# Merging triangular inverses with narrow products and stacked transfers, and a norm tail with its root on ScalarE

## The chip, the cores and the metric

The kernel runs on 1 core of one Trainium2 chip. The metric is the device time of one execution in microseconds. Time before: 1188.06 us, the median of 3 runs (1185.7 to 1188.26).

A core has TensorE (PE, with its weight loads shown apart as PEld), VectorE (DVE), ScalarE (ACT), GpSimd (POOL) and SyncE (SP). SP and ACT also issue the DMA transfers, each from a queue of its own, in program order.

## The reference, cut to what matters

One layer of an encoder for 1024 tokens of width 1024 in float32: a norm, one wide projection, a mixer of two halves (gated DeltaNet with 4 heads of 128, and a short gated convolution), an output projection, a second norm, a SwiGLU of width 2816, and a final norm. Two places of it matter here. The first is the inverse in the chunked delta rule (chunk = 64):

```python
lmat = jnp.where(strict, jnp.einsum('bhncd,bhnmd->bhncm', k_beta, k) * decay, 0.0)
tmat = lax.linalg.triangular_solve(lmat, eye, left_side=True, lower=True, unit_diagonal=True)
u = jnp.einsum('bhncm,bhnme->bhnce', tmat, v_beta)
w = jnp.einsum('bhncm,bhnmd->bhncd', tmat, k_beta * jnp.exp(g)[..., None])
```

`tmat` is the inverse of a unit lower triangular 64x64 matrix, one for each head and chunk (4 heads x 16 chunks). The second is the end of the kernel, the final norm:

```python
y = x32 * lax.rsqrt(jnp.mean(x32 * x32, axis=-1, keepdims=True) + RMS_EPS)
```

## The kernel before, in words

**Order of the work.** Up to the output projection of the first 512 tokens the order is set by a planner inside the kernel (`Sim`, lines 298 to 523). Tasks run as coroutines with priorities (`PR`, line 43); each asks for an operation, and the planner hands operations out by its own cost table and the time at which it expects their data, with 0.6 us added for PE (`MARGIN`, line 41). `ecopy` and `dma2` let it choose between ACT and DVE, or SP and ACT. The result is a fixed order for each engine. PE's background work is `fill` (line 939): dense products 128x128 by 128x512 in three passes, called `acc` here, whose three PSUM banks other tasks evict. All smaller work is put between them. Behind the planner the order is written out by hand: the rest of the output projection, the SwiGLU and its down projection by a seven-product scheme (`dn`), and the tail.

**The inverses.** Tokens are handled in two halves of 512 (`hf`), each as 4 tiles of 128 tokens, so two chunks of 64 to a tile. For each head `stage_a` (line 1096) forms `kk`, k times k transposed, scales and masks it into `L` (128 x 4 x 128), and sends the four 32x32 diagonal blocks of each tile to DRAM (`dl`). `gdn` (line 1214) reads all blocks back with one block to a partition (64 partitions, 32x32 each, tile `A`), inverts them on DVE by 30 steps of two operations (the elimination), and writes the inverses to DRAM (`dx`, lines 1234 to 1243). Then `merge` (line 1176) runs for each head. It reads the inverse blocks into the diagonal of a tile `xbd` that was zeroed once, in four transfers, one for each strip r of 32 rows; transposes it block by block on DVE into `Tt`; and completes the 64x64 inverses. With `L` masked to its lower left quarters (line 1136), P is `L` times `Tt`, Q is `xbd` times P, and Q is added to `Tt`: eight float32 products of 128 columns for each head, and one copy of P from PSUM. Then come u and w from the reference with `Tt`, and the scan over chunks (A, K and O), which carries the state S from chunk to chunk, and `output` (y).

**Pool slots.** Tiles with the tags `A` and `qs` have one slot each, used in turn by the blocks, their scratch, and the scan's V and q tiles. The four `xbd` tiles are reused later for weights of the output projection (`take_lx`, line 1381).

**The tail.** In the last down-projection chunk (`LASTC`), `add_out` (line 2045) adds each finished 128x512 product to `xo`, and for a finished half row takes the sum of squares on ACT. Once both halves of a tile are there, POOL (DVE for the last tile) adds them, POOL raises the sum to the power -0.5, and `final` (line 2064) scales both halves by it and by the norm weights `nfb`, and stores them. For tile 7, the last, the weights of one half are multiplied in early and its scaling is done on ACT; everything else is scaled on DVE and stored from SP. `settle` (line 2080) puts each `final` two products behind its add, and what is left at the end is flushed in order: tile 6, then tile 7.

Of the kernel before, what the change touches and what calls it, by code (L numbers as in the profile page):

```python
# [17 lines left out]
P = 128  # L18
# [35 lines left out]
def kernel(  # L54
# [79 lines left out]
    def flat(ap):  # L134
        return ap.rearrange("p a b -> p (a b)")
# [4 lines left out]
    def bc1(row, n):  # L140
        return row.unsqueeze(1).to_broadcast([row.shape[0], n, row.shape[1]])
# [50 lines left out]
    def dma(out, in_):  # L192
        SP.dma_start(out=out, in_=in_)

    def dma2(out, in_):
        kw = dict(out=out, in_=in_)
        mover[0].either([("sp", "dma_start", nc.sync.dma_start, (), kw), ("act", "dma_start", nc.scalar.dma_start, (), kw)])
# [898 lines left out]
    def stage_a(hf, h, dl, T, dec):  # L1096
        st = sc_[hf]
        sim.wait(lambda: all((x, h, hf) in done for x in "kq") and h in dec)
        qk = qkT[h, hf]
        kv_, qv = qk[:, 0, :], qk[:, 1, :]  # L1100
        hcol = lambda n: st[n][:, :, h]
        at, L, WQ, egl = (dec[h][n] for n in ("at", "L", "WQ", "egl"))
        kt = gt("kt")
        qd = WQ[:, :, 64:192]
        pk = bank(chb, "kT")
        for t in range(4):
            tr(pk[:, tsl(t)], kv_[:, tsl(t)])
        ecopy(flat(kt), pk)
        ss = gt("ss", (P, 2, 4))
        junk = gt("jk", (P, P), BF16)  # L1110
        for t in range(4):
            ACT.activation(junk, pk[:, tsl(t)], AF.Square, accum_out=ss[:, 0, t:t + 1])
        free(pk)
        pkk = bank(chb, "kk")
        for t in range(4):
            mm(pkk[:, tsl(t)], kv_[:, tsl(t)], kv_[:, tsl(t)])
        nk, rk, av, bv, nav = (gt(t, (P, 4)) for t in ("nk", "rk", "av", "bv", "nav"))
        bk = gt("bk", (P, 4))
        DVE.tensor_scalar(nk, ss[:, 0, :], EPS, None, ALU.add)
        DVE.reciprocal(av, nk)  # L1120
        rsqrt_pow(rk, nk, 4)
        DVE.tensor_tensor(av, av, hcol("beta"), ALU.mult)
        DVE.tensor_scalar(nav, av, -1.0, None, ALU.mult)
        for t in range(4):
            DVE.scalar_tensor_tensor(L[:, t, :], pkk[:, tsl(t)], nav[:, t:t + 1], L[:, t, :], ALU.mult, ALU.mult)
        free(pkk)
        for r in range(4):
            dma(dl[h * 16 + r * 4:h * 16 + r * 4 + 4, :].rearrange("t (a b) -> a t b", a=32),
                L[32 * r:32 * r + 32, :, 32 * r:32 * r + 32])
        T[h] = dict(egl=egl, bk=bk, kt=kt, WQ=WQ, L=L, at=at, bv=bv)  # L1130
        done.add(("L", hf, h))
        DVE.tensor_tensor(bk, av, hcol("eG"), ALU.mult)
        DVE.tensor_tensor(bv, rk, hcol("beta"), ALU.mult)
        for t in (nk, rk, av, nav):
            free(t)
        DVE.tensor_tensor(L, L, bc1(offm, 4), ALU.mult)
        DVE.tensor_tensor(qd, v3(qv, 4), qd, ALU.mult)
        pqk = bank(chb, "qk")
        for t in range(4):
            mm(pqk[:, tsl(t)], kv_[:, tsl(t)], qv[:, tsl(t)])  # L1140
        DVE.tensor_tensor(sw(at), sw(v3(pqk, 4))[:, :, ::-1, :], sw(at), ALU.mult)
        free(pqk)
        pq = bank(chb, "qT")
        for t in range(4):
            tr(pq[:, tsl(t)], qv[:, tsl(t)])
        free(qk)
        live[0] -= 1
        for t in range(4):
            ACT.activation(junk, pq[:, tsl(t)], AF.Square, accum_out=ss[:, 1, t:t + 1])
        free(pq)  # L1150
        free(junk)
        nq = gt("nq", (P, 4))
        ec = EPS * 128.0
        DVE.tensor_scalar(nq[0:64, :], ss[64:128, 1, :], EPS, ec, ALU.add, ALU.mult)
        DVE.tensor_scalar(nq[64:128, :], ss[0:64, 1, :], EPS, ec, ALU.add, ALU.mult)
        free(ss)
        T[h]["nq"] = nq
        done.add(("a", hf, h))
# [14 lines left out]
        free(bv)  # L1173
        done.add(("vt", hf, h))

    def merge(hf, h, T, dx):
        st, t_ = sc_[hf], T[h]
        u = us[hf]
        for r in range(4):
            dma2(xbd[h][32 * r:32 * r + 32, :, 32 * r:32 * r + 32],  # L1180
                dx[h * 16 + r * 4:h * 16 + r * 4 + 4, :].rearrange("t (a b) -> a t b", a=32))
        Tt = gt("Tt")
        sim.wait(lambda: ("a", hf, h) in done)
        DVE.transpose(flat(Tt), flat(xbd[h]))
        pP = bank(chb, "P")
        for t in range(4):
            mm(pP[:, tsl(t)], t_["L"][:, t, :], Tt[:, t, :])
        ecopy(flat(t_["L"]), pP)
        free(pP)
        pQ = bank(chb, "Q")  # L1190
        for t in range(4):
            mm(pQ[:, tsl(t)], xbd[h][:, t, :], t_["L"][:, t, :])
        DVE.tensor_tensor(flat(Tt), flat(Tt), pQ, ALU.add)
        free(pQ)
        DVE.tensor_tensor(t_["L"], t_["kt"], bc2(t_["bk"], P), ALU.mult)
        free(t_["bk"])
        sim.wait(lambda: ("vt", hf, h) in done)
        pu = bank(chb, "u")
        for t in range(4):
            mm(pu[:, tsl(t)], Tt[:, t, :], u[:, h, t, :])  # L1200
        ecopy(flat(u[:, h]), pu)
        free(pu)
        pw = bank(chb, "w")
        for t in range(4):
            mm(pw[:, tsl(t)], t_["L"][:, t, :], Tt[:, t, :])
        free(t_["L"])
        free(Tt)
        ecopy(t_["WQ"].rearrange("p t (c n) -> p t c n", c=4)[:, :, 0:4:3, :],
                 pw.rearrange("p (t c n) -> p t c n", t=4, c=2))
        free(pw)  # L1210
        DVE.tensor_tensor(t_["kt"], t_["kt"], bc2(st["kd"][:, :, h], P), ALU.mult)
        done.add(("uw", hf, h))

    def gdn(hf):
# [28 lines left out]
        dma(dx, flat(A))  # L1243
        free(A)
        free(tmp)
        for h in heads:
            sim.spawn(merge, PR["m"], hf, h, T, dx)
        sim.wait(lambda: all(("uw", hf, h) in done for h in heads))
        for h in heads:
            sim.spawn(zload, PR["out"], hf, h)  # L1250
# [130 lines left out]
    def take_lx(n):  # L1381
        def take():
            sim.wait(lambda: all(("uw", 1, h) in done for h in heads))
            return gt("L", (P, HT), F32R), gp.tile([P, HT], F32R, name=nm("wu"), tag=f"xbd{n}", bufs=1)
        return take

    def take_wq():
# [29 lines left out]
    def coordinator():  # L1417
# [10 lines left out]
        s_ctx.__exit__(None, None, None)  # L1428
        pools["g"] = tc.tile_pool(name="gp", bufs=2, side="left", reuse_waits="tile")
        gp = pools["g"].__enter__()  # L1430
        for i in range(4):
            xbd.append(gp.tile([P, 4, P], F32, name=f"xbd{i}", tag=f"xbd{i}", bufs=1))
        for t in xbd:
            POOL.memset(t, 0.0)
        done.add("gp")
        sim.wait(lambda: "filled" in done and live[0] == 0 and all(("vt", 1, h) in done for h in heads) and
                 all(("sc", i, hf) in done and ("z", i, hf) in done for i in range(4) for hf in range(2)))
# [580 lines left out]
    block(NP, 0)  # L2018
    first_mats(3, "B21", None)
    block(NP, 1)  # L2020
    flush()
    xq_ctx.__exit__(None, None, None)
    dq = ctx.enter_context(tc.tile_pool(name="dq", bufs=1, side="right", reuse_waits="tile"))
# [21 lines left out]
    def add_out(ci, s, i, ps):  # L2045
        an = STEPSD[s][1]
        hf, ch = ADDS[an]
        t = 4 * hf + i
        cs = slice(ch * HT, (ch + 1) * HT)
        DVE.tensor_tensor(xo[t][:, cs], xo[t][:, cs], ps, ALU.add)  # L2050
        if ci < LASTC or an not in ("A12", "S4", "S3", "A22"):
            return
        st = fst[t]
        junk = dp.tile([P, HT], BF16, name=nm("jf"), tag="jf", bufs=2)
        ACT.activation(junk, xo[t][:, cs], AF.Square, scale=1.0 / 32.0, accum_out=st[:, ch:ch + 1])
        if an in ("A12", "S3"):
            POOL.tensor_scalar(st[:, ch:ch + 1], st[:, ch:ch + 1], EPS, None, ALU.add)
            if t == NT - 1:
                DVE.tensor_tensor(xo[t][:, cs], xo[t][:, cs], nfb[:, cs], ALU.mult)
        else:  # L2060
            (DVE if t == NT - 1 else POOL).tensor_tensor(st[:, 2:3], st[:, 0:1], st[:, 1:2], ALU.add)
            rsqrt_pow(st[:, 3:4], st[:, 2:3], 1)

    def final(t):
        for ch in (1, 0):
            cs = slice(ch * HT, (ch + 1) * HT)
            dst = outs[t * P:(t + 1) * P, cs]
            if t == NT - 1 and ch == 1:
                ACT.activation(xo[t][:, cs], xo[t][:, cs], AF.Copy, scale=fst[t][:, 3:4])
                ACT.dma_start(out=dst, in_=xo[t][:, cs])  # L2070
            else:
                DVE.scalar_tensor_tensor(xo[t][:, cs], xo[t][:, cs], fst[t][:, 3:4], nfb[:, cs], ALU.mult, ALU.mult)
                dma(dst, xo[t][:, cs])
# [6 lines left out]
    def settle(k):  # L2080
        while adds and adds[0][0] <= k:
            _, (ci, s, i), ps = adds.pop(0)
            add_out(ci, s, i, ps)
            if ci == LASTC and STEPSD[s][1] in ("S4", "A22"):
                finals.append((k + 2, 4 * ADDS[STEPSD[s][1]][0] + i))

    for k, (n, i) in enumerate(slots):
        ci, s = seq_d[n]
# [62 lines left out]
```

## Time and profile before

| what | value |
|---|---|
| median of the runs | 1188.06 us (1185.7 to 1188.26) |
| the profiled execution's own time | 1187.97 us |
| its span in the trace | 1186.2 us |
| granted TensorE clock over the span | 0.996 |
| PE busy | 99% of the span |
| DVE, ACT, POOL busy | 78%, 45%, 5% |
| first merge of the inverses, first P product | 205.8 us |
| second merge, first P product | 388.8 us |

A row of a timeline has the start in us, the length in us, engine, line, operation, output<-input and the count; in brackets stands the idle time before it and what ended it. A row of a tile view has the shortest, middle and longest duration in ns and the first and last start. `SPq` and `ACTq` are DMA issues on those engines. Lines 91, 92 and 442 are helpers that record every operation, so groups are told apart by their tiles.

### The profile page before, as it was taken

Reading aid. Unit: us, or ns where it says so; the run is one execution under the profiler, and the core shown is the slowest. Engines: PE = TensorE matmul, PEld = TensorE weight load, DVE = VectorE, ACT = ScalarE, POOL = GpSimd, SP = SyncE. Lnnn points to the kernel's source line nnn. Section 1 sums busy time; section 2 is a strip of 40 time slices with the busy share of each in tenths; the row PEclk is TensorE's granted clock in tenths of the full one; section 3 lists DMA queues with packets and bytes.
Section 4 is the critical chain, followed back from the end, with each engine's and each line's share of the span. In section 5 each row is a group of like instructions: output and inputs, shape, how many; then the busy total and the mean of one; then the engine's idle time right before and its main releaser. Section 6 shows DMA issues by size and latency. Waiting matters only on the chain.

```text
span 1186.2 us, 16777 instructions
## 1 busy us (share of the span) xinstructions
PE 1175.4 (99%) x5721; PEld 987.9 (83%) x5721; DVE 929.5 (78%) x1719; ACT 528.9 (45%) x1127; POOL 58.0 (5%) x95
## 2 busy tenths in 40 slices
PE   9999999999999999999999999999999999999997
PEld 8888888988888888888888888888888888888886
DVE  5998888799998798758787677767767697788676
ACT  4479832458642444224443333333333364433343
POOL 2010100001100001100000000000000000000003
PEclk8999999999999999999999999999999999999999
DMA  9942355544344535722354655455644679869413
GB/s 295 270 108 64 99 172 142 183 119 135 109 127 124 169 102 174 283 92 87 129 172 135 221 195 172 152 182 187 221 153 137 223 272 394 312 201 344 146 38 142
DMA packets 175791, 207.08 MB, mean 175 GB/s; under 512 B 21845, under 2 KB 107994, under 8 KB 175706
## 3 DMA queue, kind: packets, MB, share of 16 engines
q1 hardware_dynamic: 170328, 202.85, 52.8%
q10 hardware_dynamic: 5378, 3.16, 0.9%
q8 instruction: 45, 0.74, 0.3%
q14 instruction: 40, 0.33, 0.1%
HBM read 150.91 MB, written 55.05 MB: 174 GB/s over the span
## 4 chain that ended last, share of the span: by engine, by line
PE 96%; DVE 2%; DMA 1%; ACT 1%; issue 0%; POOL 0%; DVEq 0%; ACTq 0%; SPq 0%; POOLq 0%
PE acc L91 34%; PE acc L442 26%; PE dn L91 17%; PE o L91 4%; PE o L442 4%; PE A L442 1%; PE K L442 1%; PE ada L442 1%; PE tr L442 1%; PE ab L442 1%; PE u L442 1%; PE w L442 1%; PE qk L442 1%; PE kk L442 1%; PE O L442 1%; PE heat L91 1%
## 5 line engine op out<-in xcount | busy, mean ns | idle before, releaser
L442 PE MATMUL acc<-h,u 128*128 128x512 f32 x1200 | 300.3, 398 | 0.0
L442 PEld LDWEIGHTS acc<-h,u 128*128 128x128 f32 x1200 | 219.0, 188 | 41.7
L91 PE MATMUL acc<-h,hl 128*128 128x512 f32 x600 | 140.1, 390 | 0.0
L91 PEld LDWEIGHTS acc<-h,hl 128*128 128x128 f32 x600 | 112.4, 188 | 23.2
L91 PE MATMUL acc<-h,u 128*128 128x512 f32 x456 | 106.1, 389 | 0.0
L91 PE MATMUL acc<-T,hl 128*128 128x512 f32 x432 | 101.3, 390 | 0.2 <-ACT cc L92 0.2
L91 PEld LDWEIGHTS acc<-h,u 128*128 128x128 f32 x456 | 85.6, 188 | 17.8
L91 PEld LDWEIGHTS acc<-T,hl 128*128 128x128 f32 x432 | 80.9, 188 | 17.2 <-ACT cc L92 0.6
L92 DVE TENSOR_TENSOR xo<-xo,dn 128x512 f32<-128x512 f32 x84 | 57.2, 686 | 44.0 <-PE dn L91 35.5
L91 PE MATMUL dn<-h,h 128*128 128x512 f32 x396 | 90.7, 389 | 0.0
L91 PEld LDWEIGHTS dn<-h,h 128*128 128x128 f32 x396 | 74.3, 188 | 15.4
L92 ACT COPY cc<-acc 128x512 f32<-128x512 f32 x66 | 38.5, 591 | 108.4 <-PE acc L91 108.4
L91 PE MATMUL acc<-T,u 128*128 128x512 f32 x360 | 84.0, 389 | 0.0
L91 PEld LDWEIGHTS acc<-T,u 128*128 128x128 f32 x360 | 67.6, 188 | 14.0
L442 ACT CAST u<-raw 128x512 fp32r<-128x512 f32 x67 | 41.3, 622 | 63.6 <-PE acc L442 57.5
L92 DVE TENSOR_TENSOR cc<-cc,acc 128x512 f32<-128x512 f32 x66 | 43.9, 684 | 29.8 <-PE acc L91 29.8
L92 DVE TENSOR_TENSOR hl<-R,hl 128x512 fp32r<-128x512 f32 x60 | 39.5, 689 | 33.4 <-ACT hl L92 33.4
L442 DVE TENSOR_TENSOR u<-raw,u 128x512 fp32r<-128x512 f32 x82 | 56.2, 685 | 8.8 <-ACT u L442 8.2
L442 DVE SCALAR_TENSOR_TENSOR cv<-pr,cols_b,cv 128x512 f32<-128x512 f32 x72 | 52.9, 746 | 1.4 <-ACT cv L442 1.1
L92 ACT CAST h<-rw 128x512 fp32r<-128x512 f32 x57 | 32.7, 618 | 41.7 <-PE dn L91 34.6
L92 DVE TENSOR_TENSOR u<-R,u 128x512 fp32r<-128x512 f32 x46 | 30.1, 688 | 20.5 <-ACT u L92 20.5
L92 ACT CAST hl<-R 128x512 fp32r<-128x512 f32 x60 | 35.5, 620 | 23.8 <-DVE R L92 10.7
(339 smaller groups left out, 2033.5 us busy)
## 6 DMA issues: line engine op xcount, KB each, us to landing
raw<-in_w_in_dram SPq DMA_DIRECT2D x82, 256.0 KB, 3.4
am_scr<-cc SPq DMA_DIRECT2D x77, 256.0 KB, 4.9
raw<-in_w_ada_dram SPq DMA_DIRECT2D x56, 256.0 KB, 3.5
rw<-am_scr SPq DMA_DIRECT2D x55, 256.0 KB, 5.1
rw<-bm_scr SPq DMA_DIRECT2D x53, 256.0 KB, 5.2
bm_scr<-raw SPq DMA_DIRECT2D x51, 256.0 KB, 5.4
R<-in_w_gate_dram SPq DMA_DIRECT2D x22, 512.0 KB, 3.8
R<-in_w_up_dram SPq DMA_DIRECT2D x22, 512.0 KB, 5.1
```

The costliest lines, as they stand in the source:

```text
L91: return call(*a, **k)
L92: ins = call(*a, **k)
L442: ins = call(*a, **k)
```

## The change

It has two parts. **The merge.** The blocks in `dl` and `dx` are laid out by strip r first, then head, then tile, so that one transfer takes one strip of all heads. `xbd` is one tile for all heads (16 blocks of 128), filled by four transfers. A second tile `XA`, zeroed each time, gets the same inverse blocks, moved by 32 rows or columns, so that it pairs the blocks of two tiles of a head; a third, `DD`, gets the right-hand blocks as a stack of 32 columns and is transposed block by block on DVE. In `L` the lower left quarters of every second tile are moved beside those of its neighbour. Then only the missing quarter is computed, with 32 moving columns: P is two products for each head, Q two. Four small copies for each head place Q's quarters in `Tt`, where an add over the whole tile was before. Ten transfers replace sixteen in each half. **The tail.** For tiles 6 and 7 the root is taken on ACT with the two sums as input and bias, and the reciprocal on DVE; the table for the root is loaded early by a dummy call; half of tile 6 is scaled on ACT too, between the last add and the last square; and tile 6 is finished around tile 7's add.

```diff
@@ stage_a
         for r in range(4):
-            dma(dl[h * 16 + r * 4:h * 16 + r * 4 + 4, :].rearrange("t (a b) -> a t b", a=32),
+            dma(dl[r * 16 + h * 4:r * 16 + h * 4 + 4, :].rearrange("t (a b) -> a t b", a=32),
                 L[32 * r:32 * r + 32, :, 32 * r:32 * r + 32])
...
-        DVE.tensor_tensor(L, L, bc1(offm, 4), ALU.mult)
+        DVE.tensor_tensor(L[:, 1:4:2, :], L[:, 1:4:2, :], bc1(offm, 2), ALU.mult)
+        for c in range(2):
+            ecopy(L[64 * c:64 * c + 32, 1:4:2, 64 * c + 32:64 * c + 64], L[64 * c + 32:64 * c + 64, 0:4:2, 64 * c:64 * c + 32])
@@ merge
-    def merge(hf, h, T, dx):
+    def merge(hf, h, T, XA, DD):
...
-        for r in range(4):
-            dma2(xbd[h][32 * r:32 * r + 32, :, 32 * r:32 * r + 32],
-                dx[h * 16 + r * 4:h * 16 + r * 4 + 4, :].rearrange("t (a b) -> a t b", a=32))
+        L = t_["L"]
+        sim.wait(lambda: ("a", hf, h) in done)
+        pP = bank(chb, "P")
+        for g in range(2):
+            mm(pP[:, 32 * g:32 * g + 32], L[:, 2 * g + 1, :], DD[:, 1, 2 * h + g, :])
+        ecopy(DD[:, 0, 2 * h:2 * h + 2, :], v3(pP[:, 0:64], 2))
+        free(pP)
         Tt = gt("Tt")
-        sim.wait(lambda: ("a", hf, h) in done)
-        DVE.transpose(flat(Tt), flat(xbd[h]))
-        pP = bank(chb, "P")
-        for t in range(4):
-            mm(pP[:, tsl(t)], t_["L"][:, t, :], Tt[:, t, :])
-        ecopy(flat(t_["L"]), pP)
-        free(pP)
+        DVE.transpose(flat(Tt), flat(xbd[0][:, 4 * h:4 * h + 4, :]))
         pQ = bank(chb, "Q")
-        for t in range(4):
-            mm(pQ[:, tsl(t)], xbd[h][:, t, :], t_["L"][:, t, :])
-        DVE.tensor_tensor(flat(Tt), flat(Tt), pQ, ALU.add)
+        for g in range(2):
+            mm(pQ[:, 32 * g:32 * g + 32], XA[:, 2 * h + g, :], DD[:, 0, 2 * h + g, :])
+        for p in range(2):
+            for c in range(2):
+                q = 64 * c + 32 - 32 * p
+                ecopy(Tt[64 * c:64 * c + 32, p:4:2, 64 * c + 32:64 * c + 64], v3(pQ[q:q + 32, 0:64], 2))
         free(pQ)
+        done.add(("q", hf, h))
@@ gdn, behind the elimination and the store of dx
+        DD = gt("qs", (P, 2, 8, 32))
+        for c in range(2):
+            r0 = 32 * c + 16
+            dma(DD[64 * c:64 * c + 64, 0], dx[r0:r0 + 16, :].rearrange("(h p) (a b) -> (p a) h b", p=2, a=32))
+        XA = gt("A", (P, 8, P))
+        POOL.memset(XA, 0.0)
+        for r in range(4):
+            dma2(xbd[0][32 * r:32 * r + 32, :, 32 * r:32 * r + 32], dx[r * 16:r * 16 + 16, :].rearrange("t (a b) -> a t b", a=32))
+        for c in range(2):
+            for p in range(2):
+                q, r0 = 64 * c + 32 - 32 * p, 32 * c + p
+                dma2(XA[q:q + 32, :, q:q + 32], dx[r0:r0 + 15:2, :].rearrange("t (a b) -> a t b", a=32))
+        DVE.transpose(flat(DD[:, 1]), flat(DD[:, 0]))
         for h in heads:
-            sim.spawn(merge, PR["m"], hf, h, T, dx)
+            sim.spawn(merge, PR["m"], hf, h, T, XA, DD)
+        sim.wait(lambda: all(("q", hf, h) in done for h in heads))
+        free(XA)
+        free(DD)
@@ before the down projection
     block(NP, 1)
+    ACT.activation(warm, ones[:, 0:1], AF.Sqrt)
     flush()
@@ add_out (tail)
+        if ci == LASTC and an == "A22" and t == NT - 1:
+            DVE.reciprocal(fst[t - 1][:, 3:4], fst[t - 1][:, 2:3])
         DVE.tensor_tensor(xo[t][:, cs], xo[t][:, cs], ps, ALU.add)
+        if ci == LASTC and an == "A22" and t == NT - 1:
+            final(t - 1, (1,))
...
         if an in ("A12", "S3"):
             POOL.tensor_scalar(st[:, ch:ch + 1], st[:, ch:ch + 1], EPS, None, ALU.add)
+            if t >= NT - 2:
+                DVE.tensor_tensor(xo[t][:, cs], xo[t][:, cs], nfb[:, cs], ALU.mult)
+        elif t >= NT - 2:
             if t == NT - 1:
-                DVE.tensor_tensor(xo[t][:, cs], xo[t][:, cs], nfb[:, cs], ALU.mult)
+                final(t - 1, (0,))
+            ACT.activation(st[:, 2:3], st[:, 0:1], AF.Sqrt, bias=st[:, 1:2], scale=1.0)
+            if t == NT - 1:
+                DVE.reciprocal(st[:, 3:4], st[:, 2:3])
         else:
-            (DVE if t == NT - 1 else POOL).tensor_tensor(st[:, 2:3], st[:, 0:1], st[:, 1:2], ALU.add)
+            POOL.tensor_tensor(st[:, 2:3], st[:, 0:1], st[:, 1:2], ALU.add)
             rsqrt_pow(st[:, 3:4], st[:, 2:3], 1)
@@ final
-            if t == NT - 1 and ch == 1:
+            if t >= NT - 2 and ch == 1:
                 ACT.activation(xo[t][:, cs], xo[t][:, cs], AF.Copy, scale=fst[t][:, 3:4])
-                ACT.dma_start(out=dst, in_=xo[t][:, cs])
+                (ACT if t == NT - 1 else SP).dma_start(out=dst, in_=xo[t][:, cs])
```

The other lines of the diff make `xbd` one tile of the same total size, let its later use for weights follow, and keep tile 6 out of the list that flushes `final`.

More of the change, by code (lines that the diff above doesn't have):

```diff
@@ L1383, in take @@
             sim.wait(lambda: all(("uw", 1, h) in done for h in heads))
-            return gt("L", (P, HT), F32R), gp.tile([P, HT], F32R, name=nm("wu"), tag=f"xbd{n}", bufs=1)
+            if len(xbd) == 1:
+                xbd.append(gp.tile([P, 4, HT], F32R, name="wu", tag="xbd", bufs=1))
+            return gt("L", (P, HT), F32R), xbd[1][:, n, :]
         return take
@@ L1430, in coordinator @@
         gp = pools["g"].__enter__()
[L1431 to L1434, printed above, removed]
+        xbd.append(gp.tile([P, 16, P], F32, name="xbd", tag="xbd", bufs=1))
+        for i in range(2):
+            POOL.memset(xbd[0][:, 8 * i:8 * i + 8, :], 0.0)
         done.add("gp")
@@ L2057, in add_out, with final @@
             POOL.tensor_scalar(st[:, ch:ch + 1], st[:, ch:ch + 1], EPS, None, ALU.add)
+            if t >= NT - 2:
+                DVE.tensor_tensor(xo[t][:, cs], xo[t][:, cs], nfb[:, cs], ALU.mult)
+        elif t >= NT - 2:
             if t == NT - 1:
-                DVE.tensor_tensor(xo[t][:, cs], xo[t][:, cs], nfb[:, cs], ALU.mult)
+                final(t - 1, (0,))
+            ACT.activation(st[:, 2:3], st[:, 0:1], AF.Sqrt, bias=st[:, 1:2], scale=1.0)
+            if t == NT - 1:
+                DVE.reciprocal(st[:, 3:4], st[:, 2:3])
         else:
-            (DVE if t == NT - 1 else POOL).tensor_tensor(st[:, 2:3], st[:, 0:1], st[:, 1:2], ALU.add)
+            POOL.tensor_tensor(st[:, 2:3], st[:, 0:1], st[:, 1:2], ALU.add)
             rsqrt_pow(st[:, 3:4], st[:, 2:3], 1)
-    def final(t):
-        for ch in (1, 0):
+    def final(t, chs=(1, 0)):
+        for ch in chs:
             cs = slice(ch * HT, (ch + 1) * HT)
             dst = outs[t * P:(t + 1) * P, cs]
-            if t == NT - 1 and ch == 1:
+            if t >= NT - 2 and ch == 1:
                 ACT.activation(xo[t][:, cs], xo[t][:, cs], AF.Copy, scale=fst[t][:, 3:4])
-                ACT.dma_start(out=dst, in_=xo[t][:, cs])
+                (ACT if t == NT - 1 else SP).dma_start(out=dst, in_=xo[t][:, cs])
             else:
@@ L2084, in settle @@
             if ci == LASTC and STEPSD[s][1] in ("S4", "A22"):
-                finals.append((k + 2, 4 * ADDS[STEPSD[s][1]][0] + i))
+                t = 4 * ADDS[STEPSD[s][1]][0] + i
+                if t != NT - 2:
+                    finals.append((k + 2, t))
     for k, (n, i) in enumerate(slots):
```

## Prediction

> **What bounds the kernel now.** I read the page first (busy shares and the chain that ended last), then busy time by stage.
>
> ```profile
> span 1186.2 us, 16777 instructions
> PE 1175.4 (99%) x5721; PEld 987.9 (83%) x5721; DVE 929.5 (78%) x1719; ACT 528.9 (45%) x1127; POOL 58.0 (5%) x95
> PE 96%; DVE 2%; DMA 1%; ACT 1%; issue 0%; POOL 0%; DVEq 0%; ACTq 0%; SPq 0%; POOLq 0%
> ```
>
> PE is busy 1175.4 of 1186.2 us and makes up 96% of the chain. A busy PE need not be a fast one, so the question for each stage is whether anything but PE's own queue sets its length (columns: stretch, its length, then busy us and instructions of PE, PEld, DVE, ACT, POOL, granted clock, DMA share, GB/s):
>
> ```profile
> 200.00:220.00 20.00, 20.00 (x148) 18.72 (x147) 16.49 (x27) 6.23 (x11) 1.48 (x2) 1.00 0.54 157
> 220.00:380.00 160.00, 160.00 (x852) 136.41 (x852) 146.21 (x347) 89.21 (x246) 12.24 (x11) 1.00 0.45 127
> 380.00:410.00 30.00, 29.39 (x196) 26.33 (x196) 22.09 (x38) 13.59 (x24) 0.96 (x1) 1.00 0.62 176
> 541.00:575.00 34.00, 33.84 (x191) 28.88 (x190) 29.23 (x46) 20.07 (x38) 0.77 (x2) 1.00 0.49 162
> 575.00:1176.00 601.00, 601.00 (x2653) 497.51 (x2652) 440.82 (x668) 232.53 (x426) 7.46 (x19) 1.00 0.57 196
> 1176.00:1186.20 10.20, 2.77 (x13) 1.95 (x11) 5.38 (x9) 2.40 (x7) 2.76 (x4) 0.82 0.45 165
> ```
>
> Both merges (200 to 220 and 380 to 410) lie where PE has no idle time, but for 0.61 us in the second, and PE stays full behind them. So a PE instruction less is time less, as long as what it waits for comes no later. After 1176 PE is done; the last 8 us are add, norm, scale and store.
>
> **PE work removed.** Each merge computes P and Q for four heads.
>
> ```profile
> 203.76 2.20 PE L442 MATMUL acc<-h,u 128*128 128x512 f32 x9
> 205.81 1.95 PE L442 MATMUL P<-Tt,L 128*128 128x128 f32 x16
> L442 PE MATMUL P<-Tt,L x64: 270/275/377, 205.8 to 400.7; 128*128 128x128 f32 x64
> L442 PE MATMUL Q<-L,xbd x64: 272/275/377, 208.5 to 403.5; 128*128 128x128 f32 x64
> 104.32 0.59 PE L442 MATMUL G<-g,ct 128*128 128x16 f32 x4
> 104.76 0.71 PE L442 MATMUL acc<-h,u 128*128 128x512 f32 x2
> ```
>
> The trace has two instructions for one f32 product: 64 for the 32 P products, 64 for Q. Sixteen span 1.95 us and one lasts 0.275, so they follow each other every (1.95 - 0.275)/15 = 0.112 us. The change has half as many products, each with 32 moving columns instead of 128. What does a narrow one cost? Nearest row: G, with 16 columns, takes 104.76 - 104.32 = 0.44 us for four, 0.11 each. So width gives nothing and count gives everything: 64 instructions fewer x 0.112 = **7.1 us** less PE time, half of it in each merge. A dense product (acc) takes (205.81 - 203.76)/9 = 0.228.
>
> [...]
>
> **Transfers and their order.** The inverted 32x32 blocks go to DRAM (dx) and come back.
>
> ```profile
> 197.30 0.47 SPq L442 DMA_DIRECT2D dx<-A  x1
> 200.31 5.57 SPq L442 DMA_DIRECT2D xbd<-dx  x9
> 200.51 4.70 ACTq L442 DMA_DIRECT2D xbd<-dx  x7
> 200.34 0.95 POOL L442 MEMSET A<- 128x1024 f32 x1 [47.65 <-DMA dx<-A]
> 204.63 0.71 DVE L442 STREAM_TRANSPOSE Tt<-xbd 128x512 f32<-128x512 f32 x1 [1.50 <-DMA xbd<-dx]
> 379.57 0.47 SPq L442 DMA_DIRECT2D dx<-A  x1
> 382.49 7.14 SPq L442 DMA_DIRECT2D xbd<-dx  x8
> 388.80 3.40 PE L442 MATMUL P<-Tt,L 128*128 128x128 f32 x24
> 394.70 1.16 PE L442 MATMUL Q<-L,xbd 128*128 128x128 f32 x8 [0.48 <-ACT L L442]
> L442 SPq DMA_DIRECT2D xbd<-dx x17: 302/360/635, 200.3 to 389.2; - x17
> DMA packets 1043, 0.18 MB, mean 182 GB/s; under 512 B 880, under 2 KB 1043, under 8 KB 1043
> DMA packets 597, 0.07 MB, mean 69 GB/s; under 512 B 597, under 2 KB 597, under 8 KB 597
> ```
>
> Sixteen transfers of 128 pieces of 128 bytes become ten: two (DD) of 512 pieces, four (xbd) of 512, four (XA) of 256. That is 4096 pieces against 2048. The two packet rows are single microseconds: 1043 between 202 and 203, when the queues had a backlog, and 597 between 205 and 206. The latter is what two queues can issue: 128 pieces every 0.360 us is 356 per us and queue. With 512 pieces to an issue that limit goes, so I take the former pace.
>
> In the instruction order of the changed kernel P stands 5 dense products earlier in the first merge (behind 647 instead of 652), so at 205.81 - 5 x 0.228 = 204.67, and Q behind eight P products and one dense one, at 204.67 + 16 x 0.112 + 0.23 = 206.7. In the second merge P stands behind 1252 instead of 1240, with 3.55 us of PE already saved: 388.80 - 3.55 + 12 x 0.228 = 388.0, Q at 390.0. The last kk there moves from 1005 to 1014, so the elimination behind it and dx come 3.55 - 9 x 0.228 = 1.5 us earlier; dx lands near 381.0 instead of 382.5.
>
> First merge: dx lands at 200.3 (POOL's memset waited for just that). DD goes first on SP, with two 256 KB loads queued ahead of it instead of three. Even after the 3.4 us that the first xbd transfer needed here (200.31 to the transpose that waited for it, less one shorter load) it is in by about 203.9. DD's transpose has half the elements of the 0.71 us one, about 0.4, so P is ready at 204.4 and just meets PE. All 4096 pieces at 1043 per us, from about 202, are in by 205.9, ahead of Q at 206.7. XA must first be cleared on POOL, 0.95 us behind dx, which is done at 201.3, before its queue slot comes. Second merge: 7 us from dx to P, 9 to Q: no wait. I take 0.3 us of new waiting in the first merge and let the 0.48 us wait of Q go: together nothing. The bounds are in the rivals.
>
> Queued behind: on ACT the four XA and xbd issues stand ahead of the P copies, and the last XA on each queue waits until DD has landed; before, ACT stood behind seven such issues (4.70 us), now four. On DVE four xbd transposes and a dense eviction stand behind DD's; three banks of dense results give that eviction more than 24 x 0.228 = 5.5 us. One weight load on SP moves behind six transfers; its cast comes some 18 us later.
>
> **Small work.**
>
> ```profile
> L442 DVE TENSOR_TENSOR Tt<-Tt,Q x8: 681/681/689, 209.7 to 403.8; 128x512 f32<-128x512 f32 x8
> L442 ACT COPY L<-P x8: 579/586/603, 206.9 to 401.1; 128x512 f32<-128x512 f32 x8
> L442 ACT COPY S<-K 128x128 f32<-128x128 f32 x4 | 0.8, 280 | 2.1 <-PE K L442 2.1
> L442 ACT ACTIVATE kd<-raw 128x16 f32<-128x16 f32 x2 | 0.4, 217 | 0.5 <-DVE raw L442 0.5
> ```
>
> DVE loses eight adds (8 x 0.68 = 5.4 us) and half of eight maskings; ACT gains 32 copies of 64 elements for Q and 16 for L, each between 0.217 and 0.280, and its P copies shrink from 0.586 to the same: about 48 x 0.23 - 8 x 0.35 = 8 us more on an engine that is 45% busy. In the merge one head's four Q copies take 0.9 us; head by head PE needs 8 x 0.112 = 0.9 for u and as much for w. So ACT keeps up, hidden behind PE. If it did not, PE would wait some 0.2 us for each head.
>
> **The tail.**
>
> ```profile
> 1177.47 1.41 DVE L92 SCALAR_TENSOR_TENSOR xo<-xo,fst,nfb 128x512 f32<-128x512 f32 x2
> 1178.80 0.69 DVE L92 TENSOR_TENSOR xo<-xo,dn 128x512 f32<-128x512 f32 x1
> 1179.59 0.63 ACT L92 ACTIVATE jf<-xo 128x512 bf16<-128x512 f32 x1 [1.21 <-DVE xo L92]
> 1180.65 0.99 POOL L92 TENSOR_TENSOR fst<-fst,nhalf 128x1 f32<-128x1 f32 x1 [1.07 <-DVE fst L92]
> 1180.49 2.07 DVE L92 SCALAR_TENSOR_TENSOR xo<-xo,fst,nfb 128x512 f32<-128x512 f32 x3
> 1181.67 0.72 ACT L92 ACTIVATE xo<-xo,fst 128x512 f32<-128x512 f32 x1 [1.36 <-POOL fst L92]
> 1181.26 1.66 SPq L92 DMA_DIRECT2D out_dram<-xo  x3
> L442 ACT ACTIVATE b1c<-ada,cols_a 128x1 f32<-128x1 f32 x8 | 2.0, 252 | 0.0
> L442 DVE RECIPROCAL av<-nk 128x4 f32<-128x4 f32 x8 | 1.4, 172 | 0.0
> ```
>
> Now the three scalings on DVE end at 1182.56 and the last store is issued then. After the change tile 6's reciprocal (0.17) precedes the last add, which moves by 0.1 to 1179.6; ACT scales half of tile 6 from 1179.0 to 1179.7, so the square starts at 1179.7 instead of 1179.59. Its sum is out at 1180.4; root 0.25, reciprocal 0.17, hand-overs 0.1: 1180.9. Then ACT and DVE scale tile 7 side by side, DVE with one scaling instead of three behind the add: done by 1181.65. The last issue comes 1182.56 - 1181.65 = **0.9 us** earlier. Bounds: 0.6 if the root costs more, 1.2 if the last stores also gain from two that left sooner.
>
> **Sum.** 1187.97 (the profiled execution: span 1186.2 and 1.77 around it) - 7.1 - 0.9 = 1180.0. The median of the runs shown is 1188.06, 0.09 more, which I leave out.
>
> **Rivals.**
> *A, pieces at 597 per us* (for it: the only row with 128-byte pieces alone): 6.9 us from 201.7, so 208.6; Q waits 1.9 us in the first merge, nothing in the second (381.0 + 1.4 + 6.9 = 389.3, before 390.0). 1181.9, and up to 1185 if DD or loads get in the way of each other. 0.14.
> *B, slower: pieces at the mean pace of before.* 2048 pieces took from 200.31 to about 206.8, 315 per us, and 382.49 to 389.63 in the second, 287. 4096 at that pace need 13.0 and 14.3 us: XA lands at 213.3 and 395.3, Q waits 6.6 and 5.3 us, 11.9 in all: 1191.9. It decides from the point where the waits pass 8.0 us, a pace below some 380 per us. Against it: the 1043 row, and that issuing set that mean. 0.08. [...]
> *C, priced by columns*: if 32 columns cost a quarter of 128, the 64 instructions left save 64 x 0.084 = 5.4 more: 1174.6. The G row is against it. 0.03. [...]
> *D, hidden*: another engine holds the stages. DVE is 146.21 of 160 us busy between the merges, and if its queue set the pace the 7.1 us would be lost: 1187.1. Against it: DVE loses about as much work, and PE shows no wait there. 0.07.
>
> **How the numbers follow.** Forecast 1180.0 with 0.68 (1178 to 1182: tail and price bounds, 0.5 us of waits, and the runs' own scatter); A 0.14, B 0.08, C 0.03, D 0.07. The range leaves out B, C and D, 0.18: 1178.0 to 1185.5. Faster by over 0.2% (about what a measurement of this kernel can tell): forecast, A and C, 0.85; D within it, 0.07; B slower, 0.08.
>
> **What would show it.** P and Q at 32 instructions each, still 0.11 apart; PE busy near 1168; no idle before P or Q over 0.5 us; the last POOL power gone and the last store issued about 2.9 us after PE's end instead of 3.8. A wait of Q for XA over 2 us, or DD's transpose waiting past 205, would make it wrong.

## The result and the profile after

The changed kernel takes 1185.05 us in the median of its 22 runs, the kernel before 1186.26 on the same chips. Two of the 22 were disturbed (1891 and 4199 us); without them the median is 1184.78 and the mean 1184.5, against a mean of 1186.7 before: ratio 0.9981, 95% interval 0.9974 to 0.9989. It is faster, but by 2.2 us where 8.0 were forecast.

The page of the changed kernel, in the lines that answer to those of before:

```profile
span 1183.6 us, 16666 instructions
PE 1171.5 (99%) x5657; PEld 982.9 (83%) x5657; DVE 924.8 (78%) x1720; ACT 536.3 (45%) x1174; POOL 57.3 (5%) x92
```

PE has 64 instructions less, as forecast, but is busy 1171.5 us and not 1168. The same stages (columns as before):

```profile
200.00:220.00 20.00, 20.00 (x124) 18.73 (x123) 14.79 (x24) 9.51 (x30) 1.47 (x2) 0.83 0.64 186
...
380.00:410.00 30.00, 28.45 (x163) 25.44 (x163) 19.89 (x34) 15.80 (x41) 1.92 (x2) 0.89 0.70 182
```

Read the granted clock, third from the end: 1.00 in both merges before, 0.83 and 0.89 now. PE is full in the first merge, 20.00 of 20, and still does less. In finer stretches (stretch, length, PE busy and count, granted clock, DMA share, GB/s), at the edges of both dips:

```profile
204.00:205.00 1.00, 1.00 (x10) 1.00 0.62 236
205.00:206.00 1.00, 1.00 (x10) 0.79 0.02 6
206.00:207.00 1.00, 1.00 (x5) 0.50 0.75 272
...
212.00:213.00 1.00, 1.00 (x9) 0.79 0.87 272
```

```profile
393.00:394.00 1.00, 1.00 (x9) 0.66 0.61 194
...
400.00:401.00 1.00, 1.00 (x11) 0.93 0.00 0
```

The clock goes to exactly 0.50. The shares in the edge rows give the moments: 205.58 to 212.42 and 393.32 to 400.14, so 6.84 and 6.82 us, each losing half of itself, 3.4 us of PE's work. The timeline of the first shows what ran:

```profile
202.35 1.86 PE L442 MATMUL P<-qs,L 128*128 128x32 f32 x16
204.05 0.47 PE L442 MATMUL acc<-h,u 128*128 128x512 f32 x1
204.36 2.33 PE L442 MATMUL Q<-qs,A 128*128 128x32 f32 x16
206.51 0.77 PE L442 MATMUL acc<-h,u 128*128 128x512 f32 x1
...
207.93 1.91 PE L442 MATMUL u<-u,Tt 128*128 128x128 f32 x8
...
214.09 1.06 PE L442 MATMUL u<-u,Tt 128*128 128x128 f32 x8
```

P and Q follow each other without a gap, with one dense product between them. In the middle of Q, 3.2 us behind P's start, everything turns slow: a dense product takes 0.77 instead of 0.47, eight u instructions 1.91 instead of 1.06. PE shows no wait there. A clock that halves looks in the page like a busy PE.

The second merge has a second trouble, a wait that I had excluded:

```profile
379.62 0.49 SPq L442 DMA_DIRECT2D dx<-A  x1
383.49 1.29 SPq L442 DMA_DIRECT2D qs<-dx  x2
387.16 1.41 ACTq L442 DMA_DIRECT2D A<-dx  x2
388.61 0.62 ACT L442 CAST h<-raw 128x512 fp32r<-128x512 f32 x1 [4.48 <-DMA xbd<-dx]
389.26 0.69 DVE L442 TENSOR_TENSOR h<-raw,h 128x512 fp32r<-128x512 f32 x1 [2.88 <-ACT h L442]
389.87 0.43 DVE L442 STREAM_TRANSPOSE qs<-qs 128x256 f32<-128x256 f32 x1
390.36 1.97 PE L442 MATMUL P<-qs,L 128*128 128x32 f32 x16 [1.54 <-DVE ch L442]
```

ACT stands at its last two issues until 388.6. Behind them is a cast (h), behind the cast a subtraction on DVE, and behind that DD's transpose (qs). P starts when that transpose ends, at 390.30. DD's data was there before: its two transfers, issued at 383.5 and 384.2, took 4.1 us each, so the last landed at 388.3, and PE had no more work from 388.82 on.

The start of the kernel differs too, with nothing changed there. Before, first, then after:

```profile
16.00:18.00 2.00, 2.00 (x11) 0.50 1.12 336
```

```profile
16.00:18.00 2.00, 1.40 (x13) 1.00 1.12 335
```

Here a dip of the same depth fell in one execution and not in the other. So of the 2.6 us between the two spans, 2.2 are luck (first P at 202.35 here, at 204.51 in the experiment e1_wide, which has the start's dip and the same order up to it). The rest, by terms: products -7.1, dips 2 x 3.4 = +6.8, the wait 1.54 less the 0.61 us of idle that went = +0.9, tail -0.55; with the start -2.15. Some 0.5 us stay unassigned.

### The profile page after: what moved, and what is told of

Same layout as the page of the kernel before. It is cut to its first block, busy times and chain, and to the rows that moved or that the text cites. A ratio compares the mean times of both kernels' runs of the same rounds, so it can differ in the third digit from the quotient of the medians.

```text
span 1183.6 us, 16666 instructions
## 1 busy us (share of the span) xinstructions
PE 1171.5 (99%) x5657; PEld 982.9 (83%) x5657; DVE 924.8 (78%) x1720; ACT 536.3 (45%) x1174; POOL 57.3 (5%) x92
## 4 chain that ended last, share of the span: by engine, by line
PE 93%; DVE 4%; ACT 1%; DMA 1%; issue 1%; POOL 0%; ACTq 0%; DVEq 0%; POOLq 0%
PE acc L91 34%; PE acc L442 24%; PE dn L91 17%; PE o L91 4%; PE o L442 3%; PE K L442 1%; PE A L442 1%; PE u L442 1%; PE ada L442 1%; PE w L442 1%; DVE xo L92 1%; PE ab L442 1%; PE qk L442 1%; PE kk L442 1%; PE heat L91 1%
```

## The experiments

My theory after this comparison: the narrow products themselves cost the clock, and after some 3 us of them it is halved (0.50, from 3.2 us behind the first P's start and 3.0 us behind the second's). Rivals: the new transfers and waits do it, or the tail carries the whole gain.

| kernel | median us | ratio (95% interval) | clock of the profiled run |
|---|---|---|---|
| after | 1184.78 | 0.9981 (0.9974 to 0.9989) | 0.993 |
| e1_wide | 1180.74 | 0.995 (0.9936 to 0.9964) | 0.996 |
| e2_tail | 1186.88 | 1.0003 (0.9994 to 1.0012) | 0.997 |
| e3_merge | 1184.65 | 0.9987 (0.9974 to 1.0) | 0.995 |
| e4_before_narrow | 1189.46 | 1.0027 (1.0013 to 1.004) | 0.996 |
| e5_wide_sp | 1179.26 | 0.993 (0.9917 to 0.9942) | 0.996 |
| e6_w64 | 1182.07 | 0.996 (0.9947 to 0.9973) | 0.999 |
| e7_pwide | 1179.38 | 0.9939 (0.9926 to 0.9952) | 0.996 |
| e8_start | 1178.91 | 0.9929 (0.9916 to 0.9941) | 0.999 |
| e9_all | 1178.15 | 0.9928 (0.9917 to 0.994) | 0.999 |
| e10_all_oldtail | 1178.91 | 0.9933 (0.9921 to 0.9945) | 0.999 |
| e11_start_w64 | 1182.4 | 0.9965 (0.9951 to 0.9979) | 0.999 |
| e12_start_w32 | 1184.14 | 0.9982 (0.9973 to 0.9991) | 0.993 |

Each ratio is to the kernel before on the same chip. That kernel's median is 1185.96, 1188.07 and 1186.32 us on the three chips of the experiments, by the share of its runs that have the start's dip; its runs at a clock of 0.999 take 1185.6 to 1185.8 us in the mean on all three. A ratio carries that share. So two rows are compared by their medians, with the ratios beside them where they say something else.

### e1_wide: the same products, made wide

```diff
-            mm(pP[:, 32 * g:32 * g + 32], L[:, 2 * g + 1, :], DD[:, 1, 2 * h + g, :])
+            mm(pP[:, 128 * g:128 * g + 128], L[:, 2 * g + 1, :], bc1(DD[:, 1, 2 * h + g, :], 4))
...
-            mm(pQ[:, 32 * g:32 * g + 32], XA[:, 2 * h + g, :], DD[:, 0, 2 * h + g, :])
+            mm(pQ[:, 128 * g:128 * g + 128], XA[:, 2 * h + g, :], bc1(DD[:, 0, 2 * h + g, :], 4))
...
```

The same 32 columns are read four times over; the lines left out here let the copies read the first quarter of each result.

> The changed kernel with the products P and Q made 128 columns wide again: the same 32 columns are streamed four times (stride 0), and only the first quarter of the result is read. Instructions, order, transfers and waits stay as in the changed kernel; a product behind its own weight load takes about 0.11 us at 32 and at 128 columns. Theory 1 (narrow products keep the array idle three quarters of their time, so the granted clock falls to 0.50 in both merges for about 6.8 us each): the granted clock stays at 0.9 to 1.0 at 204 to 214 and 390 to 402 us, PE's busy time falls by 5 to 7 us against the changed kernel's 1171.5, and the time by as much, to 1178 to 1180 us, ratio 0.992 to 0.995. Rival (the missing gain lies in waits and in the ten transfers): 1184 to 1186 us, ratio 0.998 to 1.000, and the dips stay.

1180.74 us, ratio 0.995: four times the columns, and 4 us less than the changed kernel, though not quite the 1178 to 1180 us expected. Its clock and its PE rows:

```profile
206.00:208.00 2.00, 2.00 (x20) 1.00 0.45 152
...
394.00:396.00 2.00, 2.00 (x18) 1.00 0.27 88
```

```profile
204.51 1.95 PE L442 MATMUL P<-qs,L 128*128 128x128 f32 x16
206.53 1.95 PE L442 MATMUL Q<-qs,A 128*128 128x128 f32 x16
389.42 2.05 PE L442 MATMUL P<-qs,L 128*128 128x128 f32 x16 [1.71 <-DVE ch L442]
```

Both dips are gone; sixteen instructions take 1.95 us where the narrow ones took 1.86. PE's busy time is 1167.9 us, 3.6 less than after, where 5 to 7 were expected. But this execution has the start's dip, worth some 2.2 us, and that of after has not; with it the difference is 5.8. The wait before the second P stays, 1.71 us, so it is not the dips that it comes from, nor they from it. The theory holds, the rival is out. That narrow products leave the array idle for three quarters of their time is my estimate, from 32 of 128 columns in the same 0.11 us; no trace shows it.

### e4_before_narrow: the kernel before, made narrow

```diff
-            mm(pP[:, tsl(t)], t_["L"][:, t, :], Tt[:, t, :])
+            mm(pP[:, t * P:t * P + 32], t_["L"][:, t, :], Tt[:, t, 0:32])
...
-            mm(pQ[:, tsl(t)], xbd[h][:, t, :], t_["L"][:, t, :])
+            mm(pQ[:, t * P:t * P + 32], xbd[h][:, t, :], t_["L"][:, t, 0:32])
...
```

> The kernel before with all its 128 products P and Q cut to their first 32 columns (three quarters of P and of Q are left out, so the off-diagonal inverses are incomplete); transfers, order and number of instructions stay. Theory 1: the granted clock falls to 0.50 in both merges of this kernel too, where it was 1.00, for 6.8 us or more each, and the time rises by 5 to 8 us, ratio 1.004 to 1.007. Rival (width and clock have nothing to do with each other; the dips come from the new transfers or waits): the clock stays at 1.00 and the ratio is 0.998 to 1.000.

Less streamed, more time: +0.27%, 3.2 us, less than the 5 to 8 expected. The copies of P and the adds of Q are cut to the same columns, and the planner moved other work with them, which I had not expected (the second merge's first P stands at 382.02 instead of 388.80), so this is the price of the whole edit. An instruction is no faster for its width (0.276 us in the median, 0.275 before). The profiled execution has one dip, in its second merge:

```profile
384.00:386.00 2.00, 2.00 (x19) 0.96 1.08 339
386.00:388.00 2.00, 2.00 (x11) 0.50 0.69 241
...
392.00:394.00 2.00, 2.00 (x17) 0.84 0.23 85
```

By the edges 385.84 to 392.64, 6.8 us, with the old transfers and with no idle of PE from 380 to 394. So neither the new transfers nor a wait is needed. The first merge kept 1.00 here, so narrow products do not draw a dip every time; the clocks of the runs go from 0.990 to 0.997.

### e2_tail and e3_merge: each half alone

The edits are the hunks of the diff shown above, from the dummy root on for e2_tail, and all ahead of it for e3_merge.

> The kernel before with the tail's edits alone (root on ScalarE, the last two tiles' scaling taken ahead). By the prediction's step: 0.6 to 1.2 us less, ratio 0.999 to 0.9995; by the profile of the changed kernel, where the time from PE's end to the span's end fell from 7.44 to 6.89: 0.55 us, ratio 0.9995. Rival (the tail carries the whole measured difference, and the merges give nothing): 2.2 us less, ratio 0.998. The granted clock in both merges stays as in the kernel before, 1.00.

> The changed kernel without the tail's edits: the merges alone. Theory 1: both dips to 0.50 are there as in the changed kernel, so the 7 us of P and Q that went are given back, and it is 1.0 to 2.0 us faster than the kernel before, ratio 0.998 to 0.9995. Rival (the tail carries the measured difference): ratio 1.000 within 0.001. If the merges gave what the prediction said, 7 us, the ratio would be 0.994.

e3_merge has 0.9987, as expected, and e2_tail 1.0003, above the 0.999 to 0.9995 expected; their intervals hold 1.000 at an end or inside. The merges did not give 7 us, and the tail does not carry the gain. The profile of e3_merge has a dip in the second merge and none in the first, where I expected both; the section on e11_start_w64 and e12_start_w32 comes back to it. What the tail is worth these two can't tell: the runs scatter by the start's dip (kernel before on their chip: 1185.59 in the mean at a clock of 0.999, 1188.39 at 0.995). In the profile of e2_tail the span ends 6.69 us behind PE, before 7.44.

### e5_wide_sp: ScalarE freed of its issues

```diff
-            dma2(xbd[0][32 * r:32 * r + 32, :, 32 * r:32 * r + 32], dx[r * 16:r * 16 + 16, :].rearrange("t (a b) -> a t b", a=32))
+            dma(xbd[0][32 * r:32 * r + 32, :, 32 * r:32 * r + 32], dx[r * 16:r * 16 + 16, :].rearrange("t (a b) -> a t b", a=32))
...
-                dma2(XA[q:q + 32, :, q:q + 32], dx[r0:r0 + 15:2, :].rearrange("t (a b) -> a t b", a=32))
+                dma(XA[q:q + 32, :, q:q + 32], dx[r0:r0 + 15:2, :].rearrange("t (a b) -> a t b", a=32))
```

> The changed kernel with P and Q 128 columns wide (as in e1_wide) and all ten transfers of dx issued by SyncE, none by ScalarE; the planner moves some later instructions with it. Theory (in the second merge ScalarE stands behind its issues for XA, so its cast h, VectorE's subtraction h and the transpose of DD come late, and P waits 1.5 to 1.7 us): the wait before the second merge's P falls under 0.3 us and the time by 1.2 to 1.7 us against e1_wide, to 1179 to 1179.6 us, ratio 0.9935 to 0.9945. Rival (eight issues of about 0.6 to 0.9 us in a row on SyncE bring XA later, and loads queue behind them): Q or the load of raw waits instead, 1180.5 to 1182 us, ratio 0.995 to 0.9965.

1179.26 us, 1.5 less than e1_wide (2.4 by the ratios), ratio a little better than expected. In its second merge:

```profile
378.56 1.29 SPq L442 DMA_DIRECT2D qs<-dx  x2
379.90 2.21 SPq L442 DMA_DIRECT2D xbd<-dx  x4
382.20 1.91 SPq L442 DMA_DIRECT2D A<-dx  x4
383.64 0.44 DVE L442 STREAM_TRANSPOSE qs<-qs 128x256 f32<-128x256 f32 x1
```

```profile
384.98 1.95 PE L442 MATMUL P<-qs,L 128*128 128x128 f32 x16
387.00 1.95 PE L442 MATMUL Q<-qs,A 128*128 128x128 f32 x16
```

DD's transpose comes 5.1 us behind its issue instead of 6.4, P finds it done, and Q does not wait for eight issues on one queue. (The planner has moved other work as well, so the gain is that of the whole edit; the intervals of e1_wide and e5_wide_sp overlap.)

### e6_w64, e7_pwide: how narrow, and for how long

e6_w64 is e1_wide with 64 columns; e7_pwide has P as e1_wide and Q as the changed kernel.

> The changed kernel with P and Q 64 columns wide (the 32 columns streamed twice, half of the result read): a dose between 32 and 128. If a half-full array is enough for the clock, no dips in the merges and 1180 to 1181 us, ratio 0.995, as e1_wide; if it isn't, dips as in the changed kernel and 1184.5 to 1185.5 us, ratio 0.998 to 0.999; something between, if the dips come in part of the runs.

> The changed kernel with P 128 columns wide and Q left at 32: the narrow stretch is 2 us long instead of 4. [...] Rival (any narrow stretch does it): dips as in the changed kernel, 1184.5 to 1185.5 us, ratio 0.998 to 0.999.

e7_pwide is no slower than e1_wide (the intervals overlap), and faster than the rival's 1184.5 us. Its profile has 1.00 in both merges: in that execution some 2 us of narrow products (1.87 us in the first merge) drew no dip, where 4 us did in the changed kernel's. The other four runs list a clock of 0.997 or 0.998, which the start's dip can account for, so for them it is not shown. e6_w64 came out between, which left it open; e11_start_w64 settles it.

### e8_start: the same at the start

The start has 30 instructions (15 products) with one column in a row. Here each is 64 wide, and P and Q are 128 wide as in e1_wide:

```diff
-                    mm(pa[:, s_:s_ + 1], t[:, kk, s_, :], c_act[:, kk:kk + 1], kk == n0, n0 == 0 and kk == KB - 1)
+                    mm(pa[:, 64 * s_:64 * s_ + 64], t[:, kk, s_, :], c_act[:, kk:kk + 1].to_broadcast([P, 64]), kk == n0, n0 == 0 and kk == KB - 1)
...
```

The lines left out find room in PSUM for the wider results, in turn, and read one column of each.

> e1_wide with the start's one-column products ada made 64 columns wide too (the column repeated, one of the 64 results read). The kernel before and e1_wide show 0.50 at 16 to 22 us behind 30 of these products, in part of their runs. Theory (narrow products at the start do the same as in the merges): the clock stays at 1.00 at 14 to 24 us, the runs scatter less, and the median falls by 1.5 to 2.5 us against e1_wide, to 1178.3 to 1179.3 us, ratio 0.993 to 0.994. Rival (the start waits for its loads in any case, as PE's idle of 0.6 us at 17 us in the changed kernel's profile shows): 1180.7 us, ratio 0.995.

1178.91 us, as expected. The start in its profile:

```profile
16.00:18.00 2.00, 1.31 (x13) 1.00 1.09 330
```

Every run has a granted clock of 0.998 or 0.999, where the kernel before has 0.995 to 0.999; the ten runs of e9_all and e10_all_oldtail, with the same start, have it too. So much of the scatter between the runs of the kernel before is this dip, though not all: these five still spread over 2.3 us. PE's busy time is 1164.7 us, 6.8 below the changed kernel's profile, which had no dip at the start either: just the two dips.

### e11_start_w64 and e12_start_w32: the dose, without the start

With the start quiet (0.998 or 0.999 in fifteen runs), I put a loss of clock in a run down to the merges. e11_start_w64 is e8_start with 64 columns in P and Q, e12_start_w32 with 32.

> e8_start with P and Q 64 columns wide instead of 128, so that a loss of clock in a run can come from the merges alone. If 64 columns are enough: granted clock 0.998 to 0.999 in every run, 1179 us, ratio 0.993. If they are not: 0.993 to 0.996, 1181 to 1185 us, ratio 0.995 to 0.998.

> The changed kernel with the start's ada products 64 columns wide and P and Q left at 32: the merges' dips alone. Theory 1: granted clock 0.993 to 0.996 in every run (one or two dips of 3.4 us of PE's work), 1182.3 to 1185.7 us, so 3.4 to 6.8 us over e8_start; ratio 0.9955 to 0.9985. If the merges' dips were not what costs, as e8_start: 0.993.

| columns of P and Q | median us | granted clocks of the runs |
|---|---|---|
| 128 (e8_start) | 1178.91 | 0.998 once, 0.999 four times |
| 64 (e11_start_w64) | 1182.4 | 0.995, 0.996 and 0.999, three times each |
| 32 (e12_start_w32) | 1184.14 | 0.993 to 0.996, eleven runs |

From 128 to 32 columns nothing in the kernel differs but the width: 5.2 us (6.3 by the ratios, whose kernel before had the start's dip more often on the chip of e8_start). With 64 a third of the runs keeps the clock and takes 1178.92 to 1179.63; the others take 1181.81 to 1185.3, about what 32 columns take (1182.04 to 1186.61). In e12_start_w32 the edges of the two dips are:

```profile
206.00:207.00 1.00, 1.00 (x7) 0.53 0.16 59
209.00:210.00 1.00, 1.00 (x8) 0.77 0.86 287
390.00:391.00 1.00, 1.00 (x9) 0.68 0.86 266
400.00:401.00 1.00, 1.00 (x9) 0.70 0.00 0
```

206.06 to 209.46 is 3.40 us, 390.36 to 400.60 is 10.24. With the 6.84 and 6.82 of the changed kernel, these dips last one, two or three times 3.41 us. In both executions the two also start on a grid of that step: 390.36 - 206.06 = 184.30 is 54.0 times 3.413 (a third of the 10.24), and 393.32 - 205.58 = 187.74 in the changed kernel is 55.0 times. If that grid holds, it should matter how narrow products lie on that grid. In the changed kernel the step of 3.41 ahead of the first dip is 202.17 to 205.58, and narrow from 202.35 on but for one dense product. e3_merge has the same products in the same order:

```profile
202.78 1.87 PE L442 MATMUL P<-qs,L 128*128 128x32 f32 x16
204.00:206.00 2.00, 2.00 (x19) 1.00 0.63 225
...
388.00:390.00 2.00, 1.97 (x17) 0.97 1.04 335
```

Its dip starts at 389.88; counted back 54 steps of 3.413, its grid would have a step from 202.2 to 205.6. P comes 0.6 us into it, Q ends 1.1 us into the next, and the clock stays at 1.00. A wait ahead of narrow products seems to add to them: the second dip of e12_start_w32 starts 0.72 us behind P's start, which stood behind 1.92 us of waiting.

```profile
389.64 2.98 PE L442 MATMUL P<-qs,L 128*128 128x32 f32 x16 [1.92 <-DVE ch L442]
```

Behind such a wait, products of 128 columns kept 1.00 (1.71 us in e1_wide, 1.84 in e8_start). This reading of the grid rests on these executions; no run was built to test it.

In the first merge of the changed kernel there was no gap of PE at all (busy 20.00 of 20.00 us), and 3.2 us of narrow products, with one dense product between them, came ahead of the dip to 0.50. Why they halve the clock, no run here shows.

### e9_all and e10_all_oldtail

All three edits together, and the same with the old tail.

> All three together on the changed kernel: P and Q 128 columns wide, the ten transfers issued by SyncE alone, the start's ada products 64 columns wide. If the wait before the second merge's P (1.5 to 1.8 us in e1_wide and e8_start) and the start's dip are separate costs, this is 1.3 to 1.8 us faster than e8_start: 1177.1 to 1177.7 us, ratio 0.991 to 0.992. Rival (what e5_wide_sp gained was the chip's scatter or is given back by the later order): as e8_start, 1178.9 us, ratio 0.993.

> e9_all with the tail of the kernel before, so that the tail's edits are measured where the runs scatter least. By the prediction's step 0.9 us slower than e9_all (0.6 to 1.2), by the profile of the changed kernel 0.55 us; ratio 0.0005 to 0.001 higher. Rival: no difference.

e9_all has 1178.15 us, ratio 0.9928: the lowest median of all, 8.2 us (0.7%) below the kernel before (1186.32) and 0.6% below the changed one, but not measurably ahead of e8_start (1178.91, ratio 0.9929), where 1.3 to 1.8 us were expected. Its profile has no wait of PE in the second merge and a span of 1175.5 against 1177.1 us. So how much of the wait's 1.8 us comes back stays open: 0.1 by the ratios, 0.8 by the medians, 1.6 by the spans. The tail, in e9_all and in e10_all_oldtail:

```profile
1164.40 4.24 PE L91 MATMUL dn<-wu,wu 128*128 128x512 f32 x18
1171.56 0.37 ACTq L92 DMA_DIRECT2D out_dram<-xo  x1
```

```profile
1164.42 4.24 PE L91 MATMUL dn<-wu,wu 128*128 128x512 f32 x18
1172.32 0.34 ACTq L92 DMA_DIRECT2D out_dram<-xo  x1
```

PE ends at the same time, the last issue is 0.76 us earlier, and the spans (1175.5 and 1176.3) differ by 0.8, as the medians do. The intervals of the two ratios overlap, so the size rests on the profiles.

## Why the prediction was wrong, step by step

**"So width gives nothing and count gives everything": the step that failed.** Its price was right: the P and Q rows of the changed kernel have 32 instructions each, 1.86 us for sixteen.

```profile
L442 PE MATMUL P<-qs,L x32: 190/276/297, 202.3 to 392.1; 128*128 128x32 f32 x32
L442 PE MATMUL Q<-qs,A x32: 192/276/402, 204.4 to 395.4; 128*128 128x32 f32 x32
```

But width gives something after all, of the other sign: narrow products cost the clock, their own and that of what stands behind them (0.50 for 6.84 and 6.82 us in the changed kernel, 1.00 in both merges of e1_wide). The G row on which I leaned is four instructions long, 0.44 us, too short to show it. The sign was in the profile of before, at the start, where 30 instructions with one column were followed by a clock of 0.50 at 16 to 20 us; I read the granted clock from 200 us on, and there it was 1.00, with products of 128 columns. In the median the dips take back 4.0 us (e1_wide against after) to 5.2 (e8_start against e12_start_w32).

**"Second merge: 7 us from dx to P, 9 to Q: no wait": failed, 1.5 us.** I had seen that ACT stands behind its issues and that DVE has an eviction, but not the link between them: the cast h behind the issues, its subtraction on DVE, and DD's transpose behind it. ACT had five of the ten issues there, not four. dx also took 3.9 us to land (379.62 to 383.49), before 2.9. e5_wide_sp shows the place; there P waits for nothing.

**Places in the order: right.** In e1_wide, whose execution has the start's dip as that of before, P stands at 204.51 (forecast 204.67), Q at 206.53 (206.7), and the second P would have started at 389.42 - 1.71 = 387.7 (388.0). PE's busy time is 1167.9 (near 1168).

**Transfers in the first merge, rivals A and B: right to leave them.** No wait of PE before P or Q in the first merge, in either kernel; the doubled pieces cost nothing there, and the wait of Q for its copy in the second (0.48) went. (By B's own sums its waits pass 8.0 us at some 350 to 370 pieces per us, not 380; nothing hangs on it.)

**Small copies: right.** The 31 copies on ACT take 0.20 each (forecast 0.217 to 0.280), and none holds PE.

**Tail, 0.9 us: right, a little large.** In the changed kernel (PE's end, the last root and reciprocal, the last store's issue):

```profile
1172.47 4.24 PE L91 MATMUL dn<-wu,wu 128*128 128x512 f32 x18
...
1178.36 0.29 ACT L92 ACTIVATE fst<-fst 128x1 f32<-128x1 f32 x1
1178.69 0.16 DVE L92 RECIPROCAL fst<-fst 128x1 f32<-128x1 f32 x1 [0.54 <-ACT fst L92]
...
1179.64 0.37 ACTq L92 DMA_DIRECT2D out_dram<-xo  x1
```

The last issue is 1179.64 - (1172.47 + 4.24) = 2.93 us behind PE's end, as forecast (2.9), with 0.29 for the root (0.25) and 0.16 for the reciprocal (0.17). By e9_all and e10_all_oldtail the step is worth 0.76 to 0.8.

**The sum.** Forecast -8.0; dips +4.0 to +5.2, the waits +0.9 (1.54 came and 0.61 went, where I had set both together at nothing), the tail +0.1: -3.0 to -1.8. Measured -2.2 (-3.1 to -1.3 by the interval). None of my rivals had this mechanism. The range reached 1185.5 for the sake of rival A, whose wait in the first merge did not come; that the median lies inside it, near that end, is luck.

## What to carry to other kernels

An operand cut to a quarter of its columns saved next to nothing here (1.86 us for sixteen instructions against 1.95), where each instruction has a weight load of its own (5657 of both), and it cost the clock: some 4 us or more of narrow P and Q drew a dip in six of the eight merges profiled (the changed kernel, e3_merge, e4_before_narrow, e12_start_w32), some 2 us in neither of two (e7_pwide). So where narrow products in a row last longer than those 2 us, repeat their columns (stride 0) to the full width and measure; a wait ahead of them may count (1.92 us in e12_start_w32). One dense product of 0.47 us between P and Q was not enough. Read the granted clock in every stage, the start too, and ask of a dip which products came just ahead; a PE busy to 99%, as here, hides it. When a transpose or copy waits behind an issuing engine, follow the queue one engine further: issue, cast, subtraction, transpose (1.54 us of P's wait here).

## What the runs showed that I had not expected

- The clock halves with PE full and never waiting: 0.50 from 205.58 to 212.42, from 3.2 us behind the start of 32 instructions of 32 columns.
- In two executions both dips start on one grid of 3.41 us (54.0 and 55.0 steps apart), which fits that the same narrow products drew one in the changed kernel's first merge and none in that of e3_merge (0.50 and 1.00).
- Half-width is not a safe middle in the merges: 64 columns kept the clock in three runs of nine, 128 in all five. At the start, 64 kept it in all fifteen runs of e8_start, e9_all and e10_all_oldtail.
- Wider costs next to no time: 1.95 us for sixteen instructions of 128 columns, 1.86 for 32.
- The dip behind the one-column products at the start makes runs of the kernel before 2.8 us longer (1185.59 at a clock of 0.999, 1188.39 at 0.995, in the means).
